# The output projection of each layer as two 1024-column calls, with two of eight feature pairs as seven products

## The chip, the cores and the metric

One Trainium2 chip, one of its cores. The metric is the device time of one execution, in microseconds (us). Of the kernel before, three runs gave 2045.31, 2045.35 and 2046.12 us (median 2045.35). The engines are named as the profile names them: PE (TensorE matmuls), PEld (its weight loads), DVE (VectorE), ACT (ScalarE), POOL (GpSimd), SP (SyncE, which issues the weight DMAs here).

## The reference, cut to what matters

Two layers, 256 tokens, width 2048, all in float32. Each layer is a token mixer (layer 0: a spatial-gating MLP; layer 1: grouped attention with rotary positions) with four more heads that attend into 256 memory tokens. The head outputs are concatenated (2048 features) and multiplied by `w_out` (2048 x 2048); then comes a SwiGLU feed-forward part.

```python
h = rms_norm(x, g_mix[l])
tok_in, q_mem = jnp.split(h @ w_in, [...], axis=-1)
tok_out = chunked_spatial_gating(...) if l % 2 == 0 else gqa_axial_attention(...)
mem_out = memory_attention(q_mem, mem, g_mem[l], w_mem_kv[l], g_mq[l], g_mk[l])
x = x + jnp.concatenate([tok_out, mem_out], axis=-1) @ w_out[l]
x = x + swiglu(rms_norm(x, g_ffn[l]), w_gate_up[l], w_down[l])
```

## The kernel before, in words

Tokens are two groups of 128 (`t` = 0, 1), features are groups of 128 (`kc`), outputs are blocks of 512 columns. A product of one token group, one feature group and one 512-column block is done in float32 by three matmuls (`matmul3`, L196 to L200): both operands are split into a high part of reduced precision and the rest (`whi`, `wlo` of weights, L254 and L255; tiles `h` or `a` of activations), and high x high, high x low and low x high are summed in a PSUM bank of 128 x 512.

A plain call (`Linear`, L258 to L286) computes 512 columns. It fetches four feature groups of weights in one DMA of 1 MB (L268), splits them in two halves of 128x1024 (ACT, then DVE), and adds 4 x 2 products into two banks `acc`, one for each token group. In the kernel before, `w_out` is four plain calls for each layer (L735); after each, DVE adds the two banks to the residual tiles `X` (L596).

A paired call (`Pair`, L310 to L413) computes 1024 columns as two blocks `na` and `nb`. It goes through eight feature pairs (256 features each). An ordinary pair (`eight`, L381) is eight products: two feature groups, two token groups, two blocks, into the banks 2 and 3 (token group 0), then 4 and 8 (token group 1), all from the pool `acc`. A fast pair (`seven`, L367) gets the same from seven products in the manner of Strassen and Winograd: four on sums of weights and sums of activations, into the banks 1, 5, 6, 7 from the pool `m`, and three into 2, 3 and 4. It needs three sums of weights `T` (four adds on DVE, L347 to L350, the first in place), the split of `T`, and for each pair of features four sums of activations (`activation_sums`, L300). After the last fast pair `inner` (L393) reads the four `m` banks: one copy on ACT, four adds on DVE, and with `into` four more adds into `X` (L405). `outer` (L408) adds the `acc` banks at the end, two after each token group. Before the change only the feed-forward part uses `Pair`: `w_gate_up` with two or three fast pairs and `w_down` with two, one or none.

Pools set the order of much of this. `acc` and `m` have four PSUM banks each; a plain call takes two of `acc`, a paired call takes four of `acc` and, from its first fast pair until `inner`, all four of `m`. Transposes, attention scores and other small results take `m` banks too (`misc`, L81). Weight tiles are four `raw` and three each of `whi` and `wlo`. Activation tiles of 2 KB in each partition (`big`, tag `a`) come from one pool for each mixer phase (36 tiles) and one for each feed-forward phase (26 tiles, beside two `T` and four `e` tiles of their own).

Work that isn't the main stream is handed to a queue with a due time (`later`, L96). A `tick` (L99) comes after 12 matmuls of a plain call and twice in each feature pair; it runs what is due. So transposes of `X` for the next norm, attention steps and sums are put between matmuls. The instruction order on each engine then follows from a planner (`schedule_with_timeline_sim`, L844), which starts from the program's order; tiles of one pool are handed out in the order in which the program asks for them.

In layer 1 the order around `w_out` is: queries of the memory heads (L728), memory keys (`m.keys`, L571), memory values (`m.values`, L579), then `w_out`. The steps of the memory heads (`attend`, L461) are due 4, 13, 17 and 19 ticks after the query call: scores during the values call, the transposes and the weighting of values in the first ticks of `w_out`. `scaled` (L527) reads the two `acc` banks of the values call with one ACT and one DVE instruction each (L533, L534) into four `a` tiles, which it asks for behind the four tiles of the scores' exponentials (L482).

The first feed-forward call of a layer takes its first activation sums as work due 2, 4 and 6 ticks after `w_out` (L755).

Of the kernel before, what the change touches and what calls it, by code (L numbers as in the profile page):

```python
# [39 lines left out]
class Parts:  # L40


    def __init__(self):
        self.ap, self.whole = {}, {}
# [4 lines left out]
    def get(self, kc, t):  # L49
        return self.ap[kc, t]  # L50


@with_exitstack
def encoder(ctx: ExitStack, tc: tile.TileContext, x, mem, g_mix, g_ffn, w_in_a, g_v_a, w_spatial, b_spatial,
# [165 lines left out]
    def gained(tp, t, j, g, parts, keep):  # L220

        hi = keep(F32R, [P, 4, P])
        lo = keep(F32R, [P, 4, P])
        for c in range(4):
            gc = g[:, 4 * j + c:4 * j + c + 1]
            nc.scalar.activation(hi[:, c, :], v4(tp)[:, c, :], AF.Copy, scale=gc)
            nc.vector.scalar_tensor_tensor(lo[:, c, :], v4(tp)[:, c, :], gc, hi[:, c, :].bitcast(F32), ALU.mult,
                                           ALU.subtract)
            parts.put(4 * j + c, t, hi[:, c, :], lo[:, c, :])
        parts.whole[j, t] = hi, lo  # L230
# [17 lines left out]
    def halves(raw, n, step=KC4):  # L248

        hi = wp.tile([P, KC4, NB], F32R, tag="whi", name=nm("whi"))[:, :n]  # L250
        lo = wp.tile([P, KC4, NB], F32R, tag="wlo", name=nm("wlo"))[:, :n]
        for c in range(0, n, step):
            cut = slice(c, min(c + step, n))
            nc.scalar.copy(hi[:, cut], raw[:, cut])  # L254
            nc.vector.tensor_tensor(lo[:, cut], raw[:, cut], hi[:, cut].bitcast(F32), ALU.subtract)  # L255
        return [(hi[:, c, :], lo[:, c, :]) for c in range(n)]

# [51 lines left out]

    class Pair:  # L310
# [28 lines left out]
        def prepare(self, i):  # L339

            if i in self.ready:
                return
            raw = self.fetch(i)
            self.ready[i] = (raw,)
            if i in self.fast:
                T = room["p"].tile([P, KC3, NB], F32, tag="T", name=nm("T"), bufs=2)
                nc.vector.tensor_tensor(raw[:, 0], raw[:, 0], raw[:, 1], ALU.add)  # L347
                nc.vector.tensor_tensor(T[:, 0], raw[:, 0], raw[:, 3], ALU.add)
                nc.vector.tensor_tensor(T[:, 1], T[:, 0], raw[:, 1], ALU.subtract)
                nc.vector.tensor_tensor(T[:, 2], T[:, 0], raw[:, 2], ALU.add)  # L350
                self.ready[i] = raw, T

# [14 lines left out]
        def seven(self, i, raw, T):  # L367
            t1, w00, w10, w11 = halves(raw, KC4)
            t2, t3, t4 = halves(T, KC3)
# [91 lines left out]
    def attend(qn, waits, keys, values, kv_of, kc0, parts):  # L461
# [42 lines left out]
        def weigh(pr):  # L504
# [12 lines left out]
            for hh in range(2):  # L517
                for t in range(NT):
                    ts = slice(t * P, (t + 1) * P)
                    parts.put(kc0 + 2 * pr + hh, t, hi[:, hh, ts], lo[:, hh, ts])  # L520
# [65 lines left out]
    def add_residual(acc, j, norm, g, parts):  # L586

        def turn(t):
            norm_piece(X[t][j], t, j, g, parts, kept)
            norm.add(X[t][j], t, j)  # L590
            if j == 3 and t == NT - 1:
                norm.finish()

        for t in range(NT):
            if acc:
                nc.vector.tensor_tensor(X[t][j], acc[t], X[t][j], ALU.add)  # L596
            later(1 + t, lambda t=t: turn(t))

    def residual_turns(j, norm, g, parts):
        add_residual(None, j, norm, g, parts)  # L600
# [4 lines left out]
    for l in range(DEPTH):  # L605
        scope = ExitStack()
        room["p"] = scope.enter_context(tc.tile_pool(name=f"mix{l}", bufs=MIX_TILES, reuse_waits="tile"))
        cat = Parts()
        m = Memory(l)
        if l == 0:  # L610
# [93 lines left out]
            for c in range(3):  # L704
                acc = linear(hT, w, c * NB)
                for t in range(NT):
# [3 lines left out]
                    later(1 + t, lambda u=u, t=t, c=c: turn_u(u, t, c))  # L710
        else:
# [16 lines left out]
            m.attend(linear(hT, w, TOK + 2 * MEMW), norm.r, cat)  # L728
            m.keys()
# [4 lines left out]
        units = kd if l else [(12, KC4), (0, KC4), (4, KC4), (8, KC4)]  # L734
        for j in range(4):  # L735
            add_residual(linear(cat, w_out[l], j * NB, units), j, norm, gslice("ffn", l), hF)
# [4 lines left out]
        room["p"] = scope.enter_context(tc.tile_pool(name=f"ffn{l}", bufs=FFN_TILES, reuse_waits="tile"))  # L741
        sums = {}
        fast = (0, 1, 2)

        def feature_sums(i):
            j, c = i // 2, 2 * (i % 2)
            whole = []
            for t in range(NT):
                hi, lo = hF.whole[j, t]
                a = big(F32, [P, 2, P])  # L750
                nc.vector.tensor_tensor(a, hi[:, c:c + 2].bitcast(F32), lo[:, c:c + 2].bitcast(F32), ALU.add)
                whole.append(a)
            sums[i] = activation_sums(*whole)
# [6 lines left out]
        for chunk in (range(0, 4), range(4, 8), range(8, 11)):  # L760
# [17 lines left out]
            for f in chunk:  # L778
                order, some = ((3, 4, 5, 0, 6, 1, 7, 2), 2) if f == 0 else ((0, 3, 1, 4, 2, 5, 6, 7), 3)
# [18 lines left out]
            for jj, g in enumerate(pairs):  # L798
                g.run(None if jj else pairs[1])
                for j in (2 * jj, 2 * jj + 1):  # L800
                    if last and l < DEPTH - 1:
                        residual_turns(j, next_norm, gslice("mix", l + 1), hT)
# [45 lines left out]
```

## Time and profile before

| | before |
|---|---|
| median of three runs | 2045.35 us |
| the profiled execution's own time | 2045.77 us |
| its span, first to last instruction | 2044.0 us |
| PE, PEld, DVE, ACT busy | 2028.7, 1679.5, 1604.7, 1095.1 us |
| mean granted TensorE clock | 0.999 |
| HBM read | 390.26 MB |

Busy time is the union of an engine's instructions. Matmuls overlap each other in the pipeline, so their mean duration isn't the distance between them; that is read from the start times in the timeline. L12 is line 12 of the kernel; a line can be that of a helper, so one line stands for many places. The stretch of `w_out` is 231 to 321.9 us in layer 0 and 1239.4 to 1336.2 us in layer 1 of the span; the first feed-forward call follows each.

### The profile page before, as it was taken

Reading aid. Unit: us, or ns where it says so; the run is one execution under the profiler, and the core shown is the slowest. Engines: PE = TensorE matmul, PEld = TensorE weight load, DVE = VectorE, ACT = ScalarE, POOL = GpSimd, SP = SyncE. Lnnn points to the kernel's source line nnn. Section 1 sums busy time; section 2 is a strip of 40 time slices with the busy share of each in tenths; the row PEclk is TensorE's granted clock in tenths of the full one; section 3 lists DMA queues with packets and bytes.
Section 4 is the critical chain, followed back from the end, with each engine's and each line's share of the span. In section 5 each row is a group of like instructions: output and inputs, shape, how many; then the busy total and the mean of one; then the engine's idle time right before and its main releaser. Section 6 shows DMA issues by size and latency. Waiting matters only on the chain.

```text
span 2044.0 us, 24691 instructions
## 1 busy us (share of the span) xinstructions
PE 2028.7 (99%) x9298; PEld 1679.5 (82%) x9298; DVE 1604.7 (79%) x1862; ACT 1095.1 (54%) x1389; POOL 49.1 (2%) x80
## 2 busy tenths in 40 slices
PE   8999999999999999999999999999999999999999
PEld 6888888888888888888888888888888888888887
DVE  5575557998888988887666876589979899798976
ACT  7765455455444554445556665555544455444552
POOL 2010000000000000000010100000000000000000
PEclk9999999999999999999999999999999999999999
DMA  9754554655656556566556434655666555665554
GB/s 330 249 177 159 187 187 148 227 168 203 208 190 220 169 201 208 200 215 209 188 190 212 157 124 142 206 179 172 205 206 211 200 176 195 206 216 196 181 197 138
DMA packets 202432, 396.08 MB, mean 194 GB/s; under 512 B 11068, under 2 KB 11432, under 8 KB 202312
## 3 DMA queue, kind: packets, MB, share of 16 engines
q1 hardware_dynamic: 198800, 385.79, 56.4%
q0 software_dynamic: 2048, 6.42, 1.0%
q10 hardware_dynamic: 1464, 2.28, 0.3%
q8 instruction: 73, 1.20, 0.2%
q14 instruction: 47, 0.39, 0.1%
HBM read 390.26 MB, written 4.19 MB: 193 GB/s over the span
## 4 chain that ended last, share of the span: by engine, by line
PE 94%; DVE 3%; DMA 1%; issue 1%; ACT 1%; SPq 0%; DVEq 0%; ACTq 0%
PE acc L200 27%; PE acc L198 27%; PE acc L199 27%; PE m L200 4%; PE m L198 4%; PE m L199 4%; PE m L204 2%; DVE wlo L255 1%; DMA raw<-in_w_gate_up 1%; ACT whi L254 0%; PE m L500 0%; DMA x<-in_x 0%; DMA raw<-in_w_down 0%; PE m L643 0%; DVE x L413 0%
## 5 line engine op out<-in xcount | busy, mean ns | idle before, releaser
L255 DVE TENSOR_TENSOR wlo<-raw,whi 128x2048 fp32r<-128x2048 f32 (+2 forms) x465 | 836.4, 1822 | 227.0 <-ACT whi L254 224.8
L254 ACT CAST whi<-raw 128x2048 fp32r<-128x2048 f32 (+2 forms) x465 | 700.9, 1539 | 584.6 <-PE acc L199 513.3
L198 PE MATMUL acc<-whi,h 128*128 128x512 f32 x1440 | 563.6, 392 | 0.8 <-ACT whi L254 0.8
L199 PE MATMUL acc<-whi,h 128*128 128x512 f32 x1440 | 562.6, 391 | 0.0
L200 PE MATMUL acc<-wlo,h 128*128 128x512 f32 x1440 | 523.8, 392 | 1.1 <-DVE wlo L255 1.1
L198 PE MATMUL acc<-whi,a 128*128 128x512 f32 x1062 | 415.4, 392 | 0.6 <-DVE a L431 0.6
L199 PE MATMUL acc<-whi,a 128*128 128x512 f32 x1062 | 414.9, 391 | 0.0
L200 PE MATMUL acc<-wlo,a 128*128 128x512 f32 x1062 | 398.8, 391 | 0.1
L200 PEld LDWEIGHTS acc<-wlo,h 128*128 128x128 f32 x1440 | 270.6, 188 | 56.9 <-DVE wlo L255 1.9
L198 PEld LDWEIGHTS acc<-whi,h 128*128 128x128 f32 x1440 | 270.7, 188 | 55.4 <-ACT whi L254 1.2
L199 PEld LDWEIGHTS acc<-whi,h 128*128 128x128 f32 x1440 | 270.6, 188 | 55.0
L200 PEld LDWEIGHTS acc<-wlo,a 128*128 128x128 f32 x1062 | 199.7, 188 | 41.5 <-DVE wlo L255 0.5
L198 PEld LDWEIGHTS acc<-whi,a 128*128 128x128 f32 x1062 | 199.9, 188 | 41.3 <-DVE a L431 0.8
L199 PEld LDWEIGHTS acc<-whi,a 128*128 128x128 f32 x1062 | 199.9, 188 | 40.5
L254 ACT CAST whi<-T 128x1536 fp32r<-128x1536 f32 x82 | 121.4, 1481 | 143.3 <-PE acc L199 104.1
L255 DVE TENSOR_TENSOR wlo<-T,whi 128x1536 fp32r<-128x1536 f32 x82 | 143.5, 1750 | 38.8 <-ACT whi L254 38.8
L198 PE MATMUL m<-whi,a 128*128 128x512 f32 x264 | 104.2, 395 | 0.7 <-ACT whi L254 0.7
L199 PE MATMUL m<-whi,a 128*128 128x512 f32 x264 | 102.8, 390 | 0.0
L347 DVE TENSOR_TENSOR raw<-raw 128x512 f32<-128x512 f32 x82 | 56.1, 684 | 56.4 <-DMA raw<-in_w_gate_up 54.3
L200 PE MATMUL m<-wlo,a 128*128 128x512 f32 x264 | 89.6, 389 | 0.0
L192 ACT CAST a<-m 128x512 fp32r<-128x512 f32 x80 | 46.3, 586 | 50.7 <-PE m L204 32.6
L193 DVE TENSOR_TENSOR a<-m,a 128x512 fp32r<-128x512 f32 x80 | 54.0, 683 | 17.5 <-ACT a L192 17.5
(126 smaller groups left out, 1469.0 us busy)
## 6 DMA issues: line engine op xcount, KB each, us to landing
raw<-in_w_gate_up SPq DMA_DIRECT2D x352, 512.0 KB, 4.7
raw<-in_w_down SPq DMA_DIRECT2D x176, 512.0 KB, 5.2
raw<-in_w_out SPq DMA_DIRECT2D x32, 1024.0 KB, 5.1
raw<-in_w_in_a SPq DMA_DIRECT2D x24, 1024.0 KB, 5.3
raw<-in_w_in_b SPq DMA_DIRECT2D x24, 1024.0 KB, 5.2
raw<-in_w_mem_kv SPq DMA_DIRECT2D x16, 1024.0 KB, 5.2
raw<-in_w_in_a SPq DMA_DIRECT2D x7, 512.0 KB, 6.1
x<-in_x SPq DMA_DIRECT2D x8, 256.0 KB, 5.7
```

The source lines that it names most:

```text
L192: nc.scalar.copy(hi, src)
L193: nc.vector.tensor_tensor(lo, src, hi.bitcast(F32), ALU.subtract)
L198: nc.tensor.matmul(out, lhsT=a[0], rhs=b[0], start=start, stop=False)
L199: nc.tensor.matmul(out, lhsT=a[1], rhs=b[0], start=False, stop=False)
L200: nc.tensor.matmul(out, lhsT=a[0], rhs=b[1], start=False, stop=stop)
L204: nc.tensor.transpose(dst[:, c * P:(c + 1) * P], src[:, c * P:(c + 1) * P], ident)
L254: nc.scalar.copy(hi[:, cut], raw[:, cut])
L255: nc.vector.tensor_tensor(lo[:, cut], raw[:, cut], hi[:, cut].bitcast(F32), ALU.subtract)
L347: nc.vector.tensor_tensor(raw[:, 0], raw[:, 0], raw[:, 1], ALU.add)
```

## The change

`w_out` becomes two paired calls for each layer, each with the feature pairs 0 and 1 as fast pairs and with an order of its own; results are added into `X` (`into`). Weight sums go to DVE as before. The sums of activations for the pairs 0 and 1 (`pair_sums`, `cat_sum`) are computed ahead of `w_out`: in layer 0 during the last two input calls (also for pair 2, which no call uses), in layer 1 with due times 2 and 10 ticks after the memory heads' query call, that is during the keys call and the values call. In the mixer phase `T` is three `a` tiles (split one by one by `halves_of`), and `e`, `v`, `f`, `y` of `inner` are four more. The norm pieces of two column blocks become due after each paired call: 1 and 2 ticks after it for the first block, 3 and 4 for the second. The order of the first gate/up call changes; its fast pairs stay at the same places.

```diff
+    def halves_of(blocks):
+        hi = wp.tile([P, KC4, NB], F32R, tag="whi", name=nm("whi"))
+        lo = wp.tile([P, KC4, NB], F32R, tag="wlo", name=nm("wlo"))
+        for c, b in enumerate(blocks):
+            nc.scalar.copy(hi[:, c], b)
+            nc.vector.tensor_tensor(lo[:, c], b, hi[:, c].bitcast(F32), ALU.subtract)
+        return [(hi[:, c, :], lo[:, c, :]) for c in range(len(blocks))]
...
+    def pair_sums(parts, i):
+        whole = []
+        for t in range(NT):
+            hi, lo = parts.two[i, t]
+            a = big(F32, [P, 2, P])
+            nc.vector.tensor_tensor(a, hi.bitcast(F32), lo.bitcast(F32), ALU.add)
+            whole.append(a)
+        return activation_sums(*whole)
...
-                T = room["p"].tile([P, KC3, NB], F32, tag="T", name=nm("T"), bufs=2)
+                if room["T"]:
+                    T = room["p"].tile([P, KC3, NB], F32, tag="T", name=nm("T"), bufs=2)
+                    T = [T, *(T[:, c] for c in range(KC3))]
+                else:
+                    T = [None, *(big() for _ in range(KC3))]
...
-            t2, t3, t4 = halves(T, KC3)
+            t2, t3, t4 = halves(T[0], KC3) if T[0] is not None else halves_of(T[1:])
...
-    def add_residual(acc, j, norm, g, parts):
+    def add_residual(wait, j, norm, g, parts):
...
         for t in range(NT):
-            if acc:
-                nc.vector.tensor_tensor(X[t][j], acc[t], X[t][j], ALU.add)
-            later(1 + t, lambda t=t: turn(t))
+            later(wait + 1 + t, lambda t=t: turn(t))
...
+                for i in ((0, 1), (2,), ())[c]:
+                    later(4 + 2 * (i % 2), lambda i=i: cat_sum(i))
...
             m.attend(linear(hT, w, TOK + 2 * MEMW), norm.r, cat)
+            for i in range(2):
+                later(2 + 8 * i, lambda i=i: cat_sum(i))
             m.keys()
             m.values()
...
-        units = kd if l else [(12, KC4), (0, KC4), (4, KC4), (8, KC4)]
-        for j in range(4):
-            add_residual(linear(cat, w_out[l], j * NB, units), j, norm, gslice("ffn", l), hF)
+        orders = ((2, 3, 0, 4, 1, 5, 6, 7), (2, 3, 0, 4, 1, 5, 6, 7)) if l else \
+            ((6, 0, 7, 1, 3, 2, 4, 5), (6, 7, 0, 3, 1, 2, 4, 5))
+        pairs = []
+        for jj in range(2):
+            into = [[X[t][2 * jj + n] for n in range(2)] for t in range(NT)]
+            fast = (0, 1)
+            pairs.append(Pair(cat, cat_sums, w_out[l], 2 * jj * NB, (2 * jj + 1) * NB, orders[jj], fast, into))
+        for jj, g in enumerate(pairs):
+            g.run(None if jj else pairs[1])
+            for n in range(2):
+                add_residual(2 * n, 2 * jj + n, norm, gslice("ffn", l), hF)
...
-                order, some = ((3, 4, 5, 0, 6, 1, 7, 2), 2) if f == 0 else ((0, 3, 1, 4, 2, 5, 6, 7), 3)
+                order, some = ((2, 3, 4, 0, 5, 1, 6, 7), 2) if f == 0 else ((0, 3, 1, 4, 2, 5, 6, 7), 3)
```

## Rows read from the trace of the kernel before

**Rows 1.** The page's part 1 (busy time, share of the span, instructions of each engine) and part 4 (the chain of work that ended last, by engine and by line).
```profile
PE 2028.7 (99%) x9298; PEld 1679.5 (82%) x9298; DVE 1604.7 (79%) x1862; ACT 1095.1 (54%) x1389; POOL 49.1 (2%) x80
...
PE 94%; DVE 3%; DMA 1%; issue 1%; ACT 1%; SPq 0%; DVEq 0%; ACTq 0%
```

**Rows 2.** The timeline of PE inside `w_out` of layer 0: start, duration, engine, line. The first and the last row are 22 products (66 matmuls) apart.
```profile
284.85 0.39 PE L198 MATMUL acc<-whi,a 128*128 128x512 f32 x1
...
285.07 0.39 PE L199 MATMUL acc<-whi,a 128*128 128x512 f32 x1
...
285.53 0.39 PE L198 MATMUL acc<-whi,a 128*128 128x512 f32 x1
...
299.81 0.39 PE L198 MATMUL acc<-whi,a 128*128 128x512 f32 x1
```

**Rows 3.** Busy time of each engine by stretch (start:end, length, then PE, PEld, DVE, ACT, POOL with their instructions, granted clock, DMA share, GB/s): `w_out` of layer 0, the first gate/up call behind it, the same two of layer 1, the last stretch ahead of `w_out` of layer 0, and 50 us of later gate/up calls.
```profile
231.00:321.90 90.90, 90.90 (x418) 75.29 (x417) 52.56 (x66) 47.13 (x84) 0.00 (x0) 1.00 0.55 184
321.90:365.80 43.90, 42.76 (x193) 35.05 (x192) 39.22 (x58) 23.34 (x29) 2.74 (x4) 1.00 0.53 180
1239.40:1336.20 96.80, 96.80 (x471) 81.12 (x470) 60.05 (x86) 52.44 (x102) 0.00 (x0) 1.00 0.50 170
1336.20:1380.50 44.30, 44.30 (x201) 36.57 (x200) 39.83 (x60) 23.81 (x31) 2.74 (x4) 1.00 0.56 189
...
187.00:231.00 44.00, 44.00 (x203) 36.45 (x202) 23.44 (x24) 19.52 (x24) 0.00 (x0) 1.00 0.54 179
...
400.00:450.00 50.00, 50.00 (x228) 41.40 (x227) 46.01 (x49) 26.22 (x24) 0.00 (x0) 1.00 0.61 205
```

**Rows 4.** DVE's groups by line and shape: busy us and mean ns of one behind the bar.
```profile
L255 DVE TENSOR_TENSOR wlo<-raw,whi 128x2048 fp32r<-128x2048 f32 x264 | 599.4, 2285 | 105.7 <-ACT whi L254 104.9
L255 DVE TENSOR_TENSOR wlo<-raw,whi 128x1024 fp32r<-128x1024 f32 x199 | 235.6, 1220 | 119.2 <-ACT whi L254 117.9 <-PE m L204 0.7
...
L347 DVE TENSOR_TENSOR raw<-raw 128x512 f32<-128x512 f32 x82 | 56.1, 684 | 56.4 <-DMA raw<-in_w_gate_up 54.3 <-DMA raw<-in_w_down 2.1
...
L400 DVE TENSOR_TENSOR e<-m,e 128x512 f32<-128x512 f32 x32 | 21.8, 682 | 0.2
...
L227 DVE SCALAR_TENSOR_TENSOR h<-m,gcol_ffn,h 128x128 fp32r<-128x128 f32 x64 | 20.6, 346 | 12.7 <-ACT h L226 12.7
...
L596 DVE TENSOR_TENSOR x<-acc,x 128x512 f32<-128x512 f32 x16 | 11.1, 692 | 15.3 <-PE acc L200 15.2
...
L751 DVE TENSOR_TENSOR a<-h,h 128x256 f32<-128x256 f32 x12 | 4.5, 416 | 0.0
L304 DVE TENSOR_TENSOR a<-a,a 128x128 f32<-128x128 f32 x15 | 4.2, 282 | 0.0
...
L255 DVE TENSOR_TENSOR wlo<-raw,whi 128x512 fp32r<-128x512 f32 x2 | 1.4, 692 | 2.0 <-ACT whi L254 2.0
```

**Rows 5.** The timeline of PE in the first gate/up calls of layer 0 and layer 1, at their interruptions (in brackets the idle time before the instruction and its releaser).
```profile
355.65 0.39 PE L199 MATMUL acc<-whi,h 128*128 128x512 f32 x1
357.18 0.50 PE L200 MATMUL acc<-wlo,h 128*128 128x512 f32 x1 [1.14 <-DVE wlo L255]
...
374.04 0.39 PE L199 MATMUL m<-whi,a 128*128 128x512 f32 x1
374.61 0.50 PE L198 MATMUL m<-whi,a 128*128 128x512 f32 x1 [0.19 <-ACT whi L254]
...
1387.61 0.40 PE L199 MATMUL m<-whi,a 128*128 128x512 f32 x1
1388.18 0.51 PE L198 MATMUL m<-whi,a 128*128 128x512 f32 x1 [0.17 <-ACT whi L254]
```

**Rows 6.** Layer 1 ahead of and in the first part of `w_out`: PE's busy time on `acc` tiles alone in one stretch (length, busy, matmuls, clock, DMA share, GB/s), then rows of the timelines of DVE and ACT.
```profile
1209.70:1239.20 29.50, 24.63 (x96) 0.94 0.32 109
...
1227.72 2.15 DVE L431 SCALAR_TENSOR_TENSOR a<-acc,s,a 128x128 f32<-128x128 f32 x8
...
1243.36 0.48 ACT L485 ACTIVATE a<-m,s 128x256 f32<-128x256 f32 x1 [2.08 <-DVE s L481]
...
1250.81 1.28 ACT L533 ACTIVATE a<-acc,mem_r 128x512 fp32r<-128x512 f32 x2
...
1251.69 0.73 DVE L534 SCALAR_TENSOR_TENSOR a<-acc,mem_r,a 128x512 fp32r<-128x512 f32 x1
...
1252.86 0.75 DVE L534 SCALAR_TENSOR_TENSOR a<-acc,mem_r,a 128x512 fp32r<-128x512 f32 x1
```

**Rows 7.** The timeline of PE in layer 1 between the keys call and the values call.
```profile
1205.43 0.28 PE L198 MATMUL m<-a,a 128*128 128x256 f32 x1
1205.55 0.28 PE L199 MATMUL m<-a,a 128*128 128x256 f32 x1
...
1208.58 0.63 PE L500 MATMUL m<-ident,a 128*128 128x128 f32 x4 [2.63 <-DVE a L490]
1209.79 0.79 PE L198 MATMUL acc<-whi,a 128*128 128x512 f32 x1 [0.58 <-DVE a L431]
...
1210.81 0.63 PE L200 MATMUL acc<-wlo,a 128*128 128x512 f32 x1
1211.23 0.63 PE L198 MATMUL acc<-whi,a 128*128 128x512 f32 x1
...
1216.89 1.03 PE L500 MATMUL m<-ident,a 128*128 128x128 f32 x8
```

More of the change, by code (lines that the diff above doesn't have):

```diff
@@ L43, in __init__ @@
     def __init__(self):
-        self.ap, self.whole = {}, {}
+        self.ap, self.two = {}, {}
     def put(self, kc, t, hi, lo):
@@ L50, in get, with put_pair @@
         return self.ap[kc, t]
+    def put_pair(self, i, t, hi, lo):
+        self.two[i, t] = hi, lo
 @with_exitstack
@@ L229, in gained @@
             parts.put(4 * j + c, t, hi[:, c, :], lo[:, c, :])
-        parts.whole[j, t] = hi, lo
+        for c in range(2):
+            parts.put_pair(2 * j + c, t, hi[:, 2 * c:2 * c + 2], lo[:, 2 * c:2 * c + 2])
     class Norm:
@@ L345, in prepare @@
             if i in self.fast:
-                T = room["p"].tile([P, KC3, NB], F32, tag="T", name=nm("T"), bufs=2)
+                if room["T"]:
[3 more added lines that the diff above has]
+                    T = [None, *(big() for _ in range(KC3))]
                 nc.vector.tensor_tensor(raw[:, 0], raw[:, 0], raw[:, 1], ALU.add)
-                nc.vector.tensor_tensor(T[:, 0], raw[:, 0], raw[:, 3], ALU.add)
-                nc.vector.tensor_tensor(T[:, 1], T[:, 0], raw[:, 1], ALU.subtract)
-                nc.vector.tensor_tensor(T[:, 2], T[:, 0], raw[:, 2], ALU.add)
+                nc.vector.tensor_tensor(T[1], raw[:, 0], raw[:, 3], ALU.add)
+                nc.vector.tensor_tensor(T[2], T[1], raw[:, 1], ALU.subtract)
+                nc.vector.tensor_tensor(T[3], T[1], raw[:, 2], ALU.add)
                 self.ready[i] = raw, T
@@ L395, in inner @@
             b, o = self.bank, self.into
-            e, v, f, y = [room["p"].tile([P, NB], F32, tag=f"e{i}", name=nm("e"), bufs=1) for i in range(4)]
+            e, v, f, y = [room["p"].tile([P, NB], F32, tag=f"e{i}", name=nm("e"), bufs=1) if room["T"] else big()
+                          for i in range(4)]
             nc.scalar.copy(e, b[1])
@@ L516, in weigh @@
             hi, lo = split(po.rearrange("p (h s) -> p h s", h=2), [P, 2, S])
-            for hh in range(2):
-                for t in range(NT):
-                    ts = slice(t * P, (t + 1) * P)
+            for t in range(NT):
+                ts = slice(t * P, (t + 1) * P)
+                parts.put_pair(kc0 // 2 + pr, t, hi[:, :, ts], lo[:, :, ts])
+                for hh in range(2):
                     parts.put(kc0 + 2 * pr + hh, t, hi[:, hh, ts], lo[:, hh, ts])
@@ L594, in add_residual @@
         for t in range(NT):
-            if acc:
-                nc.vector.tensor_tensor(X[t][j], acc[t], X[t][j], ALU.add)
-            later(1 + t, lambda t=t: turn(t))
-    def residual_turns(j, norm, g, parts):
-        add_residual(None, j, norm, g, parts)
+            later(wait + 1 + t, lambda t=t: turn(t))
     hT = Parts()
@@ L607, in encoder, with cat_sum @@
         room["p"] = scope.enter_context(tc.tile_pool(name=f"mix{l}", bufs=MIX_TILES, reuse_waits="tile"))
-        cat = Parts()
+        room["T"] = False
+        cat, cat_sums = Parts(), {}
         m = Memory(l)
+        def cat_sum(i):
+            cat_sums[i] = pair_sums(cat, i)
         if l == 0:
@@ L650, in turn_u @@
                 hi, lo = split(v4(tp), [P, 4, P])
+                for i in range(2):
+                    cat.put_pair(2 * c + i, t, hi[:, 2 * i:2 * i + 2], lo[:, 2 * i:2 * i + 2])
                 for i in range(4):
@@ L728, in encoder @@
             m.attend(linear(hT, w, TOK + 2 * MEMW), norm.r, cat)
+            for i in range(2):
+                later(2 + 8 * i, lambda i=i: cat_sum(i))
             m.keys()
@@ L741, in encoder @@
         room["p"] = scope.enter_context(tc.tile_pool(name=f"ffn{l}", bufs=FFN_TILES, reuse_waits="tile"))
+        room["T"] = True
         sums = {}
@@ L745, in feature_sums @@
         def feature_sums(i):
[L746 to L753, printed above, removed]
+            sums[i] = pair_sums(hF, i)
         for i in fast:
@@ L801, in encoder @@
                     if last and l < DEPTH - 1:
-                        residual_turns(j, next_norm, gslice("mix", l + 1), hT)
+                        add_residual(0, j, next_norm, gslice("mix", l + 1), hT)
                     elif last:
```

## The prediction

> **What bounds the kernel now.** The page comes first: PE is busy 99% of the span and carries 94% of the chain that ended last, DVE 3%, DMA and ACT 1% each [rows 1]. Busy time overstates what a matmul costs, because they overlap. So the timeline of PE is next: a 128x512 matmul lasts 0.39 us, but starts 0.22 to 0.23 us after the one before, and 22 products span 299.81 - 284.85 = 14.96 us: 0.68 us for a product of three matmuls, 0.227 for one [rows 2]. The third view is the busy time by stretch. In `w_out` DVE has room: 52.6 us of 90.9 in layer 0, 60.1 of 96.8 in layer 1. In the gate/up calls, which already use fast pairs, it hasn't: 39.2 of 43.9 us right behind `w_out`, 46.0 of 50 us later, with PE at 100% there all the same [rows 3]. The timeline of PE behind `w_out` shows where DVE is late now: one stop of 1.53 - 0.23 = 1.3 us at 355.65, and short ones of about 0.35 us at 374 and 1388 [rows 5]. So what shortens PE's work counts in full, until a bank, a tile or DVE is late.
>
> **What is removed.** Each fast pair saves one product. Two layers, two calls, two pairs: 8 products x 0.68 = **5.44 us**. Transposes, weight bytes and the other products stay. By the Trainium skill ("TensorE: Matmul & The Clock Gate", Back-to-back issue gap) matmuls of 512 columns in a stream of weight loads come every 131 ns; the 24 matmuls would then give an estimated 3.1 us. The rows have 227 ns for just such a stream, and they decide.
>
> **DVE's work in `w_out`, for each layer** [rows 4]. Gone: 32 splits of 128x1024 at 1.220 (39.0) and 8 residual adds at 0.692 (5.5). New: 16 splits of 128x2048 at 2.285 (36.6), 12 splits of 128x512 at 0.692 for `T` (8.3), 16 weight sums at 0.684 (10.9), 8 adds in `inner` and 8 of it into `X` at 0.682 (10.9), 8 adds in `outer` at about 0.69 (5.5). That is 27.7 us more. Eight norm pieces at 0.346 (2.8 us) move out to the gate/up call, since the third block's now come after the last `w_out` call too. DVE so has 52.6 + 27.7 - 2.8 = 77.5 us in a stretch of 90.9 - 2.7 = 88.2 (88%) in layer 0, and 60.1 + 24.9 = 85.0 of 94.1 (90%) in layer 1. The gate/up calls run at 92% of DVE without loss [rows 3], so I take 0 for the mean load; the cover is PE's own work, and if it fails a layer loses what DVE lacks, some us at most. Below zero there is nothing to gain here, as PE has no stop in this stretch now. ACT has half its time free [rows 3], which covers its larger splits. The sums of activations cost 2 x 0.416 + 4 x 0.282 + a split of 0.68 = 2.6 us of DVE each; three of them in layer 0 lie in calls where DVE is busy 23.4 of 44 us [rows 3]: 0.
>
> **The start of `w_out` in layer 0.** The first call needs four `acc` banks. The last input call's two are read by ACT alone, at once. I take 0.3 us for its start and its changes between slow and fast pairs (from 0 to the 1.3 us of the stop in rows 5).
>
> **The start of `w_out` in layer 1.** Here the change adds a wait. A plain call used the two banks of the keys call, which DVE had read by 1227.72 + 2.15 = 1229.9 us. The values call has 96 matmuls and ends at 1239.2 [rows 6]; its own banks are read by L533 and L534 only at 1250.81 to 1252.86 + 0.75 = 1253.6 us. That was harmless: no call needed them before the second block. Now the first feature pair needs them for token group 1, half a pair (4 x 0.68 = 2.7 us) after its start, near 1242. L533 came late although its banks were full, because its four tiles are asked for behind those of the scores' exponentials, the first of which ran at 1243.36 [rows 6]; this reading is from the program's order, no row names the releaser. The two sums of activations ask for five tiles each ahead of them, in the same pool, so this can only come later: by nothing where the tiles are there in time, by two sums of 2.6 us of DVE and a cast each, some 6 us, at worst. I take 1 us, as DVE has idle time among these instructions. What PE can do without the two banks: token group 0 of the pairs 2 and 3 (2 x 2.7), two products of the fast pair (1.4), the 24 short matmuls of the memory scores at 0.12 [rows 7] (2.9), 16 transposes (1.03 for eight [rows 7], 2.0): 11.7 us, until 1250.9. Queued behind the waiting matmul, in order on PE, is the rest of the call; ACT's and DVE's next splits wait for the `whi` buffers that it holds. The wait is then between 1252.4 + 1 - 1250.9 = 2.5 and 1253.6 + 1 - 1250.9 = 3.7 us: **3.1**. The ends: 0, if the planner brings L533 forward; and 15, if PE stops after half a pair and the scores (1239.2 + 2.7 + 2.9 = 1244.8), the banks come at 1253.6 and 6 us late. 3.1 is taken because the planner already mixes such matmuls of two calls.
>
> **The first gate/up call of each layer.** Its fast pairs keep their places, its first pairs need blocks that are now ready earlier. But DVE gets the 2.8 us of norm pieces in addition to its 39 us of 44 [rows 3]. At best the stops of rows 5 go (1.3 + 0.35 + 0.35 and small ones beside them: 3 us in all), at worst each call is 2.8 us longer (5.6). I take **+1.0**, nearer to the rows of layer 1, where the same load costs little.
>
> **DMA.** The same bytes in 32 more issues on SP, two for a pair instead of one; SP waits for `raw` buffers most of the time. 0.
>
> **Sum**, against the profiled execution's own 2045.77 us (span 2044.0 and 1.77 around it): -5.44 + 0.3 + 3.1 + 1.0 = -1.04, so 2044.7. The median is 0.42 below that execution, so **2044.3 us**.
>
> **Rivals.** (1) *The full gain.* The planner puts other work in the place of the wait, and less than 1 us of stops is added in all: 2045.35 - 5.44 + 0.6 = 2040.5. For it: PE now runs `w_out` without any idle time although much is late around it [rows 3, 6]. Against it: the banks are read 11 us later than the first call needs them. (2) *The bank wait decides, and it is slower.* PE stops near 1244.8 and the banks come about 10 us later, at 1255, because the sums hold the tiles up. The clock then falls to its lower level: now, after 2.63 and 0.58 us of idle time, matmuls start every 0.42 us instead of 0.227 until 1213, some 8 of them: 1.6 us [rows 7]. With 1 us for the gate/up calls: 2045.35 - 5.44 + 10 + 1.6 + 1 = 2052.5. It is slower by over 0.2% from about 9.5 us of added stops on. For it: the order of the tiles. Against it: PE's order isn't the program's. (3) *DVE becomes the bound* in both `w_out` and the calls behind it; both layers lose their 2.7 us again and 1 us more: 2047. For it: 90% and then 96% load (42 of 43.9). Against it: rows 3 at 400 to 450 us.
>
> **How the numbers follow.** 0.2% of 2045.35, about what a measurement of this kernel can tell from no change, is 4.1 us: below 2041.3 is faster, above 2049.4 slower. Forecast 0.45 (its own range 2041 to 2048, 0.03 of it faster), rival 1 0.26, rival 2 0.19, rival 3 0.10. Faster 0.29, same 0.52, slower 0.19. The range 2040 to 2051 cuts off the lower half of rival 1 and the longer waits of rival 2, about 2 in 10.
>
> **What would show it.** PE's count of matmuls falls by 24, and 0.68 us for a product stays. In layer 1 the first `acc` matmuls of token group 1 in `w_out` should have an idle time ahead of them with L534 as its releaser, 2 to 4 us near 1250; none there is rival 1, 8 or more with a granted clock below 1 is rival 2. In layer 0 `w_out` should end 2.4 us earlier, counted from its start. DVE should be near 88% to 90% in `w_out`. Stops released by `wlo` or `T` spread over both `w_out` stretches would be rival 3. The prediction is wrong if the sum of PE's stops grows by less than 1 or more than 8 us, or if they lie elsewhere.

## The result, and the profile after

The changed kernel takes 2050.32 us (median of 19 runs, 2048.65 to 2052.38), the kernel before 2045.56 us beside it (19 runs, 2044.34 to 2047.09). The ratio is 1.0023, 95% interval 1.0016 to 1.003: slower by 0.23%, about 4.8 us, where 2044.3 us had been forecast. One run of e11 below (2536.78 us, at a granted clock of 0.75) is left out as slow. The profiled execution took 2049.59 us, with a span of 2047.8 us: 3.82 us more than that of before. Parts 1 and 4 of its page answer to [rows 1]:

```profile
PE 2028.3 (99%) x9274; PEld 1676.5 (82%) x9274; DVE 1663.5 (81%) x1953; ACT 1108.9 (54%) x1390; POOL 53.0 (3%) x80
...
PE 94%; DVE 4%; ACT 1%; DMA 1%; issue 1%; SPq 0%; DVEq 0%; ACTq 0%
```

PE has the 24 matmuls less, and its busy time is the same all the same: busy time overstates what a matmul costs, so the loss has to be read from the start times. I took the distance from each matmul's start to the next one's and subtracted what it is in an unbroken stream (0.227 us for 512 columns, 0.119 for 256, 0.1085 for 128). What is left over, summed by stretch, is PE's lost time, stops and low clock together. The columns e1 to e8 are experiments that follow below. Each column is one execution:

| us lost on PE, by stretch of the span | before | after | e1 | e2 | e4 | e5 | e7 | e8 |
|---|---|---|---|---|---|---|---|---|
| 231 to 321, `w_out` layer 0 | 0.19 | 0.26 | 0.26 | 0.19 | 0.25 | 0.26 | 0.26 | 0.19 |
| 321 to 400, first gate/up calls layer 0 | 2.36 | 4.10 | 3.99 | 1.65 | 1.11 | 1.20 | 0.92 | 2.32 |
| 1190 to 1236, memory keys and values, layer 1 | 5.47 | 5.01 | 5.48 | 6.32 | 5.58 | 4.17 | 4.00 | 5.54 |
| 1236 to 1262, start of `w_out` layer 1 | 0.19 | 4.68 | 0.19 | 3.22 | 5.13 | 1.91 | 0.23 | 0.18 |
| 1262 to 1335, rest of it | 0.12 | 0.49 | 0.13 | 0.49 | 0.51 | 0.18 | 0.12 | 0.13 |
| 1335 to 1410, first gate/up calls layer 1 | 0.90 | 3.96 | 0.90 | 3.99 | 0.87 | 0.58 | 1.83 | 1.12 |

From before to after this is +0.07 in `w_out` of layer 0, 1.74 + 3.06 = +4.80 in the first gate/up calls, 4.49 + 0.37 = +4.86 in `w_out` of layer 1, and -0.45 in all other stretches together. With -5.44 for the 24 matmuls that makes +3.84, and the profiled executions differ by 3.82: no stretch is left out. That the sum closes doesn't test the 0.227 us, which is in both of its parts. Layer 0's `w_out` does: from its first matmul to the first one of the gate/up call it took 90.82 us before (231.01 to 321.83) and 87.29 after (230.58 to 317.87), with 12 matmuls of 512 columns and eight transposes less. 12 x 0.227 + 8 x 0.1085 is 3.59 us, and 3.53 came, as 0.07 more is lost. By the Trainium skill ("TensorE: Matmul & The Clock Gate", Back-to-back issue gap) the 24 would be worth an estimated 3.1 us; the trace, with 0.227 us from start to start, doesn't bear it out.

Busy time by stretch, columns as in [rows 3]: `w_out` and the first gate/up call of layer 0, the same two of layer 1, and four pieces around the start of `w_out` in layer 1.

```profile
231.00:320.00 89.00, 89.00 (x407) 73.50 (x406) 73.52 (x88) 50.96 (x71) 0.00 (x0) 1.00 0.57 192
320.00:364.00 44.00, 42.03 (x188) 33.51 (x187) 39.49 (x63) 25.10 (x41) 4.69 (x4) 1.00 0.50 169
1238.00:1334.00 96.00, 93.72 (x441) 77.45 (x440) 78.80 (x108) 55.30 (x89) 0.00 (x0) 0.98 0.52 171
1334.00:1379.00 45.00, 43.16 (x195) 34.49 (x194) 40.59 (x65) 26.77 (x46) 4.69 (x4) 1.00 0.45 145
1244.00:1248.00 4.00, 4.00 (x27) 3.59 (x26) 2.35 (x8) 2.04 (x8) 0.00 (x0) 1.00 0.00 0
1248.00:1252.00 4.00, 1.85 (x14) 1.23 (x13) 2.72 (x10) 3.06 (x10) 0.00 (x0) 1.00 0.00 0
1252.00:1256.00 4.00, 3.87 (x13) 2.90 (x12) 4.00 (x7) 2.07 (x5) 0.00 (x0) 0.57 0.00 0
1256.00:1260.00 4.00, 4.00 (x21) 3.33 (x20) 2.62 (x5) 1.85 (x4) 0.00 (x0) 1.00 0.28 72
```

DVE's load went from 52.6 of 90.9 us to 73.5 of 89.0 in `w_out` of layer 0, and PE still runs it without a pause. In layer 1 PE is half idle from 1248 to 1252 and then gets a granted clock of 0.57. Its timeline there:

```profile
1247.72 1.28 PE L529 MATMUL m<-ident,a 128*128 128x128 f32 x8
1250.27 0.63 PE L529 MATMUL m<-ident,a 128*128 128x128 f32 x4 [1.27 <-DVE a L519]
1251.71 0.70 PE L529 MATMUL m<-ident,a 128*128 128x128 f32 x4 [0.81 <-DVE a L519]
1252.54 0.80 PE L202 MATMUL acc<-whi,a 128*128 128x512 f32 x1
1253.14 0.63 PE L203 MATMUL acc<-whi,a 128*128 128x512 f32 x1
...
1255.27 0.53 PE L202 MATMUL acc<-whi,a 128*128 128x512 f32 x1
1255.64 0.40 PE L203 MATMUL acc<-whi,a 128*128 128x512 f32 x1
```

The same 4 us on ACT and DVE (L563 and L564 are the L533 and L534 of [rows 6]):

```profile
1249.96 0.47 ACT L514 ACTIVATE a<-m,s 128x256 f32<-128x256 f32 x1 [0.88 <-DVE s L510]
...
1250.78 0.20 ACT L514 ACTIVATION_READ_ACCUMULATOR a<-m,s 128x1 f32 x1
1250.87 1.26 ACT L563 ACTIVATE a<-acc,mem_r 128x512 fp32r<-128x512 f32 x2
```
```profile
1251.74 1.41 DVE L564 SCALAR_TENSOR_TENSOR a<-acc,mem_r,a 128x512 fp32r<-128x512 f32 x2
```

The first matmul of token group 1 starts at 1252.54, as soon as DVE has read the first of the values' two banks. Until then PE had only the transposes of the memory heads left (L529), which follow the exponentials one head at a time; hence the releaser that the rows name, L519. Their stops are 0.2 + 1.4 + 1.0 + 0.4 = 3.0 us, and seven matmuls at about 0.43 us instead of 0.227 cost another 1.5. The values' reader L563 stands on ACT right behind the last exponential.

The second place is the first gate/up call. PE in layer 0:

```profile
338.56 0.39 PE L204 MATMUL m<-wlo,h 128*128 128x512 f32 x1
339.36 0.50 PE L202 MATMUL acc<-whi,h 128*128 128x512 f32 x1 [0.41 <-ACT whi L259]
...
341.08 0.39 PE L203 MATMUL acc<-whi,h 128*128 128x512 f32 x1
341.69 0.50 PE L204 MATMUL acc<-wlo,h 128*128 128x512 f32 x1 [0.22 <-DVE wlo L260]
...
352.70 0.39 PE L203 MATMUL acc<-whi,h 128*128 128x512 f32 x1
353.91 0.73 PE L204 MATMUL m<-wlo,a 128*128 128x512 f32 x2 [0.82 <-DVE wlo L260]
...
354.94 0.40 PE L203 MATMUL acc<-whi,h 128*128 128x512 f32 x1
355.85 0.50 PE L202 MATMUL m<-whi,h 128*128 128x512 f32 x1 [0.51 <-ACT whi L259]
```

ACT and DVE ahead of the first of these stops:

```profile
337.40 1.91 ACT L259 CAST whi<-raw 128x2048 fp32r<-128x2048 f32 x1 [2.06 <-PE acc L203]
```
```profile
339.34 2.29 DVE L260 TENSOR_TENSOR wlo<-raw,whi 128x2048 fp32r<-128x2048 f32 x1 [2.44 <-ACT whi L259]
```

Four stops, 2.6 us, where [rows 5] had one of 1.3; a short one near 373 is in both kernels. Layer 1 has the same four, 2.5 us, between 1357.5 and 1374.7. Ahead of the first of them DVE *idles* for 2.44 us: it waits for ACT's cast, and that waited for a `whi` tile that PE was still reading.

### The profile page after: what moved, and what is told of

It is laid out like the page before. It is cut to its first block, busy times and chain, and to the rows that moved or that the text cites. A ratio compares the mean times of both kernels' runs of the same rounds, so it can differ in the third digit from the quotient of the medians.

```text
span 2047.8 us, 24824 instructions
## 1 busy us (share of the span) xinstructions
PE 2028.3 (99%) x9274; PEld 1676.5 (82%) x9274; DVE 1663.5 (81%) x1953; ACT 1108.9 (54%) x1390; POOL 53.0 (3%) x80
## 4 chain that ended last, share of the span: by engine, by line
PE 94%; DVE 4%; ACT 1%; DMA 1%; issue 1%; SPq 0%; DVEq 0%; ACTq 0%
PE acc L204 26%; PE acc L202 26%; PE acc L203 26%; PE m L204 4%; PE m L202 4%; PE m L203 4%; PE m L208 2%; DVE wlo L260 2%; ACT whi L259 1%; DMA raw<-in_w_gate_up 0%; DMA x<-in_x 0%; PE m L529 0%; PE m L673 0%; ACT a L514 0%; DVE x L442 0%
## 5 line engine op out<-in xcount | busy, mean ns | idle before, releaser
L202 PE MATMUL acc<-whi,a 128*128 128x512 f32 x1022 | 401.3, 393 | 0.3
L203 PE MATMUL acc<-whi,a 128*128 128x512 f32 x1022 | 399.4, 391 | 0.0
L204 PE MATMUL acc<-wlo,a 128*128 128x512 f32 x1022 | 375.7, 391 | 0.0
L204 PEld LDWEIGHTS acc<-wlo,a 128*128 128x128 f32 x1022 | 192.4, 188 | 40.3 <-DVE wlo L260 0.4
L202 PEld LDWEIGHTS acc<-whi,a 128*128 128x128 f32 x1022 | 192.6, 188 | 39.9 <-DVE a L460 0.5
L203 PEld LDWEIGHTS acc<-whi,a 128*128 128x128 f32 x1022 | 192.7, 189 | 39.1
L202 PE MATMUL m<-whi,a 128*128 128x512 f32 x296 | 116.9, 395 | 0.7 <-ACT whi L259 0.7
L203 PE MATMUL m<-whi,a 128*128 128x512 f32 x296 | 115.3, 390 | 0.0
L375 DVE TENSOR_TENSOR raw<-raw 128x512 f32<-128x512 f32 x90 | 61.8, 687 | 53.1 <-DMA raw<-in_w_gate_up 47.0
L204 PE MATMUL m<-wlo,a 128*128 128x512 f32 x296 | 101.9, 390 | 1.5 <-DVE wlo L260 1.5
L202 PEld LDWEIGHTS m<-whi,a 128*128 128x128 f32 x296 | 55.6, 188 | 15.4 <-ACT whi L259 4.6
```

What stands on the lines that cost most here:

```text
L202: nc.tensor.matmul(out, lhsT=a[0], rhs=b[0], start=start, stop=False)
L203: nc.tensor.matmul(out, lhsT=a[1], rhs=b[0], start=False, stop=False)
L204: nc.tensor.matmul(out, lhsT=a[0], rhs=b[1], start=False, stop=stop)
```

## The experiments

All ratios are to the kernel before on the same chip, five rounds each unless said otherwise.

**e1 and e2, one layer alone.** The paired calls in one layer; the other layer's `w_out`, sums and first gate/up order as before. The edit of e1; e2 has 0 in place of 1:

```diff
         for jj, g in enumerate(pairs):
+            if l == 1:
+                continue
             g.run(None if jj else pairs[1])
...
+        if l == 1:
+            for j in range(4):
+                acc = linear(cat, w_out[l], j * NB, kd)
...
```

> The paired calls in layer 0 alone; layer 1's w_out and its first gate/up call are as before the change. Theory A (the cost sits in two places, the banks at the start of layer 1's w_out with the low clock behind them, about 5 us, and the first gate/up calls, 1.7 us in layer 0 and 3.0 in layer 1): -2.7 of saved products + 0.1 + 1.7 = about 1 us faster than before (ratio 0.9995), with the stops at 338.6 to 355.9 us as in the changed kernel. Rival B (the eight feature pairs cost DVE more than PE saves in either layer alike): half of the whole loss, about 2.4 us slower than before (ratio 1.0012). Rival C (as I had predicted, the gate/up call costs only 0.5 us a layer): 1.9 us faster than before (0.9991).

> The paired calls in layer 1 alone; layer 0 is as before the change. Theory A (banks and clock 5.0, gate/up 3.0, saved products 2.7): about 5.3 us slower than before (ratio 1.0026), with the stop near 1249 to 1252.5 us and half clock until 1255. Rival B (both layers alike): 2.4 us slower (1.0012). Rival D (what layer 0 changes shifts layer 1's phases, so that the stop at the banks comes only when both are paired): no stop near 1250, less than 1 us slower.

Measured: e1 2044.76 us, ratio 0.9997 (0.9989 to 1.0006); e2 2050.26 us, 1.0023 (1.0015 to 1.0032). The loss is layer 1's. Layer 0 saves 2.72 us in `w_out` and gives back 1.63 of them in the gate/up call (3.99 against 2.36); the 1 us that is left can't be told from nothing by time. That is theory A, but for e2's low clock, which didn't come. Rival B falls, and so does D, as the stop near 1250 is there without layer 0's change. Rival C's time (0.9991) lies inside the interval of e1; its 0.5 us for the gate/up call is refuted by the trace, with 1.63. e2 shows also what the stop waits for, and something else. Its PE timeline, then the busy time behind the stop:

```profile
1252.51 0.63 PE L529 MATMUL m<-ident,a 128*128 128x128 f32 x4 [1.27 <-DVE a L519]
1253.95 0.63 PE L529 MATMUL m<-ident,a 128*128 128x128 f32 x4 [0.81 <-DVE a L519]
1254.78 0.50 PE L202 MATMUL acc<-whi,a 128*128 128x512 f32 x1 [0.20 <-DVE a L564]
1255.11 0.39 PE L203 MATMUL acc<-whi,a 128*128 128x512 f32 x1
```
```profile
1254.00:1258.00 4.00, 3.80 (x18) 3.02 (x19) 4.00 (x8) 2.31 (x5) 0.00 (x0) 1.00 0.00 0
```

Here the `acc` matmul names L564 as its releaser: the bank. And behind the same stops (1.27 and 0.81 us) the granted clock stays at 1.00.

**e3, the values' banks read early.** The memory scores are due after the values, so that L563 and L564 stand ahead of the exponentials.

```diff
-            attend(head_norm(acc, r, ghead[f"mq{self.l}"]), (4, 13, 17, 19), ...
+            attend(head_norm(acc, r, ghead[f"mq{self.l}"]), (4, 17, 18, 19) if self.l else (4, 13, 17, 19), ...
```

> The changed kernel with the due times of the memory's scores, turns and weighted sums in layer 1 moved from 13, 17, 19 to 17, 18, 19, so that the two ACT copies and DVE splits of the values (the readers of the values call's banks) stand ahead of the four exponentials on ACT and DVE, by about 6 us. No work is added or left out. Theory A (the stop at 1248.7 to 1252.5 us is the wait for those two banks): the stop of 2.8 us and the 1.8 us of low clock go, 4 to 4.6 us faster than the changed kernel, so about the time of before (0.9999 to 1.0004); something else, the turns or weighted sums, may be late by up to 1 us. Rival E (the stop is DVE's lateness in general and banks only its sign): the stop moves to another releaser in the same 10 us and less than 1.5 us is won (1.0016 to 1.0024).

Measured: 2057.53 us, ratio 1.0057 (1.0043 to 1.0071), neither theory's number. The stop at the banks went (2.25 us lost in 1236 to 1262, for a `whi`), but 10.9 us came up in the rest of `w_out`, 4.35 of it in one stop at the start of the second call and some 2.5 in low clock behind it (granted 0.50 from 1298 to 1302); the rest is shorter waits, most of them for splits. DVE, then PE there:

```profile
1291.73 2.28 DVE L260 TENSOR_TENSOR wlo<-raw,whi 128x2048 fp32r<-128x2048 f32 x1
1293.93 0.68 DVE L377 TENSOR_TENSOR a<-a,raw 128x512 f32<-128x512 f32 x1
1294.53 0.68 DVE L378 TENSOR_TENSOR a<-a,raw 128x512 f32<-128x512 f32 x1
1295.13 2.28 DVE L260 TENSOR_TENSOR wlo<-raw,whi 128x2048 fp32r<-128x2048 f32 x1
1297.33 1.28 DVE L442 TENSOR_TENSOR x<-acc,x 128x512 f32<-128x512 f32 x2
```
```profile
1298.16 0.77 PE L202 MATMUL acc<-whi,a 128*128 128x512 f32 x1 [4.19 <-DVE x L442]
```

The planner had put two splits and two weight sums, 5.6 us, ahead of the adds of `outer` (L442) that free the first call's banks. It is the bank wait again, one call later. The edit moved more than it meant to; e5 repeats it with less.

**e4, the old order in the first gate/up call.**

```diff
-                order, some = ((2, 3, 4, 0, 5, 1, 6, 7), 2) if f == 0 else ...
+                order, some = ((3, 4, 5, 0, 6, 1, 7, 2), 2) if f == 0 else ...
```

> The changed kernel with the first gate/up call's order of feature pairs as it was before (3, 4, 5, 0, 6, 1, 7, 2 in place of 2, 3, 4, 0, 5, 1, 6, 7). Theory F (the new order costs the stops of the first gate/up calls, 1.7 + 3.0 us): they fall back to those of before, 3 to 4.7 us faster than the changed kernel (ratio to before 1.0000 to 1.0008). Theory G (the stops come from DVE, which has 2.8 us more of norm pieces and 2.8 us of the last adds to do in this call): no faster, and up to 3 us slower, as blocks 2 and 3 are needed earlier in the old order and come out of the last w_out call together (1.0023 to 1.0038).

Measured: 2045.26 us, ratio 0.9997 (0.9988 to 1.0006): with the old order the whole loss of the change is gone. What PE loses in both layers' first gate/up calls fell to 1.11 and 0.87 us (before: 2.36 and 0.90). Busy time of the two first gate/up calls:

```profile
320.00:364.00 44.00, 44.00 (x202) 36.01 (x201) 42.08 (x68) 25.98 (x43) 5.65 (x4) 1.00 0.56 189
1334.00:1379.00 45.00, 45.00 (x206) 36.85 (x206) 43.62 (x68) 27.54 (x46) 5.64 (x4) 1.00 0.53 176
```

DVE is busier here than in the changed kernel (42.1 against 39.5 of 44 us), and PE loses 0.5 us in each of these stretches, where it lost 3.3 and 3.1 in the changed kernel. So DVE's load isn't what stops PE; theory G falls.

**e8, the new order without paired calls.** The same line, put the other way round, in the kernel before.

> The kernel before the change, w_out plain, with only the first gate/up call's new order of feature pairs (2, 3, 4, 0, 5, 1, 6, 7). Theory F (the order alone makes the stops, whatever w_out does): the stops of the changed kernel appear, 1.7 us more in layer 0 and 3.0 in layer 1, ratio 1.0015 to 1.0025. Rival K (the order costs only behind paired calls, whose last adds and eight norm pieces fall into this call): within 1 us of before, ratio 0.9995 to 1.0005.

Measured: 2046.03 us, ratio 1.0001 (0.9992 to 1.001); 2.32 and 1.12 us of stops, as before. Theory F falls, K holds. With e4 this makes a square: old order and plain calls, new order and plain calls, old order and paired calls each run without the loss in the gate/up calls; only new order *and* paired calls have it.

**e9 and e10, two more orders** in the changed kernel (three rounds each): 2, 4, 5, 0, 6, 1, 7, 3 and 2, 3, 4, 5, 0, 6, 1, 7.

> The changed kernel with the first gate/up call's order 2, 4, 5, 0, 6, 1, 7, 3: the old order of e4 with the pairs 2 and 3, which both need only early blocks, in each other's place. Theory L (what counts is that the pair ahead of the first fast pair is 5 and not 4, so that three ordinary pairs' splits aren't held up by the fast pair's two tiles of whi): stops in the first gate/up calls as in e4, about 1 us a layer in place of 4, ratio 1.0000 as far as these calls go (4.5 to 5 us faster than the changed kernel). Rival M (any order but the one that was there costs some us, by the planner's chance): 3 us or more a layer.

> The changed kernel with the order 2, 3, 4, 5, 0, 6, 1, 7: the new order with each fast pair one place later. Theory L: the first fast pair now follows pair 5; the stops of 0.58, 0.38, 0.98 and 0.68 us (layer 0) and their like in layer 1 go, about 1 us a layer is left, 4.5 to 5 us faster than the changed kernel. Rival N (two pairs of the early block at the front let DVE and ACT run out of work, and then too much comes at once): stops of 3 us a layer stay, at other times.

Measured: e9 2045.75 us, ratio 1.0002 (0.9993 to 1.0011), 1.16 and 0.74 us of stops: theory L. e10 2052.94 us, 1.0036 (1.0023 to 1.005): the four stops are gone, but two others of 1.05 and 1.4 us stand later, at 365.5 and 367.4 and alike in layer 1 (3.21 and 3.27 us lost in all), as rival N has it. Layer 1's start of `w_out` is worse too (7.98 us), which neither theory says. L is a rule for the first stops, then, not for the call's time. What I read from the order of the instructions: at 338.56 PE stands at pair 5, whose cast waited for the `whi` tile of pair 4, while nine matmuls of the fast pair 0 (2.0 us), all of whose operands were there, come behind it in PE's order. In e4 such matmuls of pair 0 run just while ACT makes that cast. In the changed kernel the splits of pair 0's sums, of activations and of weights, were done by 334.4 (DVE), and the first of the nine starts at 344.54 (PE):

```profile
331.13 0.68 DVE L197 TENSOR_TENSOR a<-a,a 128x512 fp32r<-128x512 f32 x1
...
332.67 1.75 DVE L260 TENSOR_TENSOR wlo<-T,whi 128x1536 fp32r<-128x1536 f32 x1
```
```profile
344.54 0.39 PE L202 MATMUL m<-whi,a 128*128 128x512 f32 x1
```

Whether their banks were free too, no row tells, and that this swap alone would do, wasn't tried.

**e5, the values first, with less moved.** On e4, scores of both pairs due at 17, turns at 18; beside the line shown, the helper `attend` is changed so that it takes a due time for each pair.

```diff
-            attend(head_norm(acc, r, ghead[f"mq{self.l}"]), (4, 13, 17, 19), ...
+            attend(head_norm(acc, r, ghead[f"mq{self.l}"]), (4, (17, 17), (18, 18), 19) if self.l else (4, 13, 17, 19), ...
```

> The kernel of e4 (the change with the old order in the first gate/up calls, 2045.26 us), with the memory's scores in layer 1 due at 17 (both pairs) and the turns at 18 in place of 13, 14 and 17, 18. On ACT and DVE the readers of the values' banks then stand ahead of the four exponentials; the order of the splits and of the adds behind them stays nearly that of e4, unlike in e3, where the last adds of the first call were put behind two splits and the second call waited 4.35 us for its banks. Theory A (stop of 2.8 us at the two banks, about 2 us of low clock behind it): 4 to 5 us faster than e4, so 2040.5 to 2041.5 us, ratio 0.9975 to 0.998. Rival E (the start of w_out in layer 1 is late for DVE's work, whoever is named): another stop of 3 us or more in 1243 to 1262, less than 1.5 us won, ratio over 0.9988.

Measured: 2042.06 us, ratio 0.9983 (0.9974 to 0.9992), faster than before. ACT, and PE behind it:

```profile
1238.31 1.28 ACT L563 ACTIVATE a<-acc,mem_r 128x512 fp32r<-128x512 f32 x2
1242.82 0.47 ACT L514 ACTIVATE a<-m,s 128x256 f32<-128x256 f32 x1 [3.23 <-DVE s L510]
```
```profile
1257.87 0.50 PE L202 MATMUL acc<-whi,a 128*128 128x512 f32 x1 [0.53 <-ACT whi L259]
...
1260.19 0.50 PE L204 MATMUL acc<-wlo,a 128*128 128x512 f32 x1 [0.67 <-DVE wlo L260]
```

The banks are read 11 us earlier than in e4 (1249.44 there). PE's loss in 1236 to 1262 falls from 5.13 to 1.91 us: two stops of 0.7 and 0.8 us for `whi` and `wlo`, no low clock. That is 3.2 us of the 4 to 5 expected. Theory A, with something else late next.

**e12, the same due times in the kernel before.**

> The kernel before the change, w_out plain, with the due times of e5 in layer 1 (scores at 17, turns at 18), so that the values' banks are read ahead of the exponentials. Theory A (only a call that needs four banks waits for the values' two): nothing to win here, the stretch 1236 to 1262 has 0.2 us of stops as before, ratio 0.9995 to 1.0005. Rival Q (the new due times relieve layer 1's start of w_out whatever the calls are, and e5's gain over e4 isn't the paired call's wait): 1 us or more faster, ratio under 0.9995.

Measured: 2045.23 us, ratio 0.9998 (0.9988 to 1.0007), 0.21 us lost in 1236 to 1262. So rival Q falls: in these kernels the readers' place matters only to a call that needs those banks at once.

**e6, the sums of activations earlier.** On e4, layer 1's two `cat_sum` are due 2 and 10 ticks from the start of the memory queries' call instead of from its end, one call earlier.

> The kernel of e4 with the two sums of activations for w_out's fast pairs in layer 1 queued one call earlier (2 and 10 ticks from the start of the memory queries' call), so that both stand ahead of the keys' head norm on DVE. Theory H (the sums, standing in DVE's and ACT's order ahead of the memory keys' transposes, delay the exponentials and the values' readers behind them by about 1 us, as I had forecast, or up to 2.6 us): the stop at the banks is 1 to 2.6 us shorter, 1 to 3 us faster than e4. Rival I (they lie in time that DVE would have idled, and the chain of scores, maxima and exponentials sets the time): the stop stays within 0.4 us, ratio 0.9997 as e4.

Measured: 2045.47 us, ratio 1.0001 (0.9992 to 1.0009). The values' banks are read at 1249.46 us (e4: 1249.44), and the stops are as large (4.86 us). Rival I: moving the sums brings nothing forward. The four heads' chain of maximum, exponential and scale stands ahead of the reader on ACT, 1.9 us for each head in the rows of e4 (its exponentials start at 1242.88, 1244.73, 1246.63 and 1248.53); that it sets the time is read from them, no run made it shorter.

**e7, plain first.** On e4, layer 1's first two column blocks as plain calls, one paired call for the others.

```diff
+        for j in range(2 * l):
+            acc = linear(cat, w_out[l], j * NB)
...
         for jj, g in enumerate(pairs):
+            if jj < l:
+                continue
```

> The kernel of e4 with the first two column blocks of layer 1's w_out as plain calls again and the other two as one paired call. Two products less are saved, 1.36 us. Theory A (the wait is for four banks at the start, and a plain call needs only the keys' two): no stop and no low clock at 1247 to 1255, so 5.0 - 1.36 = 3.6 us faster than e4, 2041.6 us, ratio 0.998. Rival J (any paired call waits at its start for four banks, as the plain call's adds into X come late too): a stop of 2 us or more at the start of the paired call near 1287, and less than 1.5 us won.

Measured: 2042.74 us, ratio 0.9983 (0.9974 to 0.9992); 0.23 us lost in 1236 to 1262 and 0.12 in the rest. Theory A; this paired call behind a plain one waits for nothing. It can't be told from e5 by time. (The profiled execution of e7, 2039.46 us, is 3.3 us under that median, so the rest of its column says little.)

**e11, a third fast pair.** On e5, `fast = (0, 1) if l else (0, 1, 2)` in `w_out`.

> The kernel of e5 with a third fast pair (2) in both of layer 0's w_out calls, for which the changed kernel already has the sums of activations. Two more products saved, 1.36 us; DVE gets 2 x (4 x 0.684 + 3 x 0.692) = 9.6 us more in w_out of layer 0, 83 of 87.6 us (95%) in place of 73.5 of 89. Theory O (DVE's mean load costs nothing in w_out as long as it stays under 100%, as I had forecast): no new stops, 1.36 us faster than e5, ratio 0.9976. Rival P (DVE becomes the bound before that): stops released by wlo or T, 1.4 us or more in 231 to 321, same time as e5 or slower.

Measured: 2051.69 us (median of five), ratio 1.0034 (1.0022 to 1.0046), about 10 us slower than e5. PE, then DVE at the start of the second call:

```profile
273.29 0.39 PE L204 MATMUL acc<-wlo,a 128*128 128x512 f32 x1
275.61 0.47 PE L202 MATMUL acc<-whi,a 128*128 128x512 f32 x1 [1.92 <-DVE x L442]
```
```profile
273.57 0.68 DVE L434 TENSOR_TENSOR x<-x,a 128x512 f32<-128x512 f32 x1
274.17 0.68 DVE L376 TENSOR_TENSOR a<-raw 128x512 f32<-128x512 f32 x1
274.78 1.28 DVE L442 TENSOR_TENSOR x<-acc,x 128x512 f32<-128x512 f32 x2
```

Busy time of layer 0's `w_out`:

```profile
231.00:320.00 89.00, 86.85 (x386) 70.80 (x385) 75.28 (x91) 50.60 (x71) 0.00 (x0) 0.98 0.55 183
```

It isn't DVE's mean load, at 75.28 of 89 us (85%). The third fast pair is the sixth of the eight, so `inner` comes later and its adds meet the end of the call, and L442 is late for the next call's banks; that is read from the order of the rows, no run moved `inner` alone. The gate/up call behind it loses 7.5 us, where e5 loses 1.2: 1.3 in a stop for L442 again, 3.7 in one for DVE's norm pieces (L231), and about 2 in low clock behind that. Rival P by its time, by another way than it says.

## Why the prediction was wrong

**Right.** -5.44 us for 24 matmuls at 0.227: the length of layer 0's `w_out` bears it out. DVE's load at no cost: in `w_out` of layer 0 it rose by 21 us (24.9 forecast; 83% and 82% of the two stretches, not 88% to 90%), and PE lost 0.07 us more. The start of layer 0's `w_out` cost 0.07 us (0.3 forecast). The place and size of the bank wait in layer 1: PE ran what the working listed, 10.6 us beyond the end of the values call (1238.02) and eight transposes more between the stops (11.7 forecast in all), and its stops are 3.0 us (3.1 forecast).

**The step that failed** is the first gate/up call of each layer: +1.0 forecast, +4.80 measured (1.74 in layer 0, 3.06 in layer 1). It said that the "fast pairs keep their places" and priced only the 2.8 us of norm pieces, against DVE's load. e4 shows that these pieces cost nothing, with DVE at 96%, and e8 that the order costs nothing by itself; the two together cost 4.8 us. How they do is shown in part only: at the first stop ACT had waited for a tile of `whi` that PE was still reading, and e9 agrees with the rule that pair 5 should stand ahead of the first fast pair, but e10 follows that rule too and loses 3.2 and 3.3 us at other places. 4.80 lies inside the bounds that the term had, 5.6 at worst, by luck: they were worked out from DVE's load, 2.8 us for a call, and layer 1 lost more than that with a cause of another kind. I took 1.0 because layer 1 of before carried the same load, when load was not what decides. Had I counted the upper end and the low clock in a case of their own, "slower" would have had more than 0.19: all that was added is 9.3 us, and 0.2% slower begins at 9.5. One of the prediction's own signs of being wrong came true: half of what PE lost lies outside `w_out`.

**Left out of the forecast** was the low clock behind the bank wait, 1.5 us. I had it in rival 2 alone, for a longer stop. [Rows 7] show it behind 2.63 + 0.58 us of idle time, and the wait I forecast was as long. These 1.5 us and the 3.8 of the step above make up the 4.9 us between the forecast (-1.04) and the measured difference (+3.84); the other terms come to -0.4.

**Wrong in the reasons, not in the size.** The sums of activations were to delay the values' readers by 1 us: with them out of the way in e6 the banks come free 14.5 us after the end of the values call (1236.65 to 1251.13), in e4 14.8 (1236.37 to 1251.12) and in the changed kernel 14.5 (1238.02 to 1252.54). So the sums cost 0.3 us at most. Before the change it was 13.2 us; the banks do come free 1.3 us later, then, but hardly for the sums. That the term of 1 us fitted is luck, and what delays the readers stays open. The order in which tiles are asked for, given there as the reason why L533 is late, is neither shown nor refuted: at run time the reader starts right behind the last exponential on ACT, without a wait of its own, so its place there holds it. Whether the tiles made the planner put it there, e5 can't tell, since it moves the scores and with them the order of asking.

Of the rivals, 2 comes nearest (2052.5, slower), by a wait of 3 us in place of its 10, and with the gate/up calls for the rest.

## What to carry to other kernels

Where a call begins to need more buffers than its predecessor, look for who reads them last and what stands ahead of that reader on its engine; putting the reader first (e5) or a call that needs fewer ahead (e7) was worth about 3 us here. With the old order in the gate/up calls it turned a loss of 0.23% into a gain of 0.17%. When two edits meet in one stretch, price and run them apart and together: in the first gate/up calls each was free here and both cost 4.8 us. After each edit compare the order of the engines' instructions with that of the kernel it came from, for an order made by a planner moves far from the edit (e3, e11).

## Not expected of the hardware

The same stops were followed by a low clock in some kernels and not in others. Busy time and granted clock (the number behind POOL's bracket) behind stops of 2.79 and 0.74 us in layer 1, between the keys and the values call, first before, then e5:

```profile
1209.00:1213.00 4.00, 3.42 (x10) 2.53 (x9) 3.64 (x15) 1.26 (x6) 1.24 (x1) 0.58 0.65 240
```
```profile
1207.00:1211.00 4.00, 3.42 (x16) 2.69 (x15) 3.21 (x13) 1.25 (x6) 1.23 (x1) 1.00 0.70 232
```

PE was busy for 3.42 us in both; at 0.58, near the lower of its two levels (1.2 of 2.4 GHz), it got 10 matmuls through, at 1.00 it got 16. The 1.5 us of low clock in the changed kernel is thus no fixed part of a 3 us stop: e2 had the stop without it. What decides wasn't tried.
